# Moving two feed-forward products ahead of the output product, with features and tokens taken in another order

## The chip, the cores and the metric

The kernel runs on one core of one Trainium2 chip. Its time is the device time of one execution in microseconds (us); a kernel's time is the median of its runs. The engines have short names here: PE (TensorE) multiplies matrices, and PEld is its loading of stationary operands; DVE (VectorE) and ACT (ScalarE) do elementwise work; POOL (GpSimd) does a little elementwise work and issues the DMAs that add to what is there; SP (SyncE) issues plain DMAs.

## What is computed

One sequence of 512 tokens with 1024 features passes through four layers. Each is a mixer (RWKV-7, windowed attention, a gated spatial unit, gated linear attention, in this order) and a feed-forward network (FFN), each behind a norm and added to the stream h; a last norm ends the program.

```
for i in range(4):
    h = h + mixer[i](rmsnorm(h, norm_mix[i]))
    h = h + swiglu(rmsnorm(h, norm_ffn[i]), ffn_w_in[i], ffn_w_out[i])
return rmsnorm(h, norm_final)

swiglu(x, w_in, w_out):  gate, up = split(x @ w_in);  (silu(gate) * up) @ w_out
```

The hidden width of the FFN is 2816. All data are float32.

## The kernel before

**Precision.** A float32 operand is split into a high part (an ACT cast, tile `whi` for weights) and a remainder (a DVE subtraction, tile `wlo`), and each product is three matmuls in a faster format: high by high, high by remainder, remainder by high (`mm3`, line 540). Weights arrive in raw tiles `wraw` (eight buffers), and there are three buffers each for `whi` and `wlo`.

**Where results lie.** h lies by token, four blocks of 128 tokens by 1024 features. A product's result lies in PSUM, which has eight banks of 128 x 512.

**The FFN.** The hidden width is cut into six blocks, four of 512 and two of 384 (`WIDTHS`, line 28), and blocks are taken in pairs (`PARTS`, line 27). For each pair, `ffn` (line 705) computes two hidden blocks (`hidden`, line 803) and then the output product that takes this pair's hidden values into h (`out_fast`, line 727). Both use `seven` (line 740), a scheme that computes a 2 x 2 block product with seven products instead of eight, out of sums of quarters of the operands. In the order in which they are written they are m1, m2, m5, m6, m3, m7, m4. Each has four token-and-feature subtiles, that is 24 matmuls in a block with four row tiles; the output product of the 384 pair has three row tiles and 18. The sums of weight quarters are made by the DMA that loads: POOL issues a DMA that adds onto a raw tile. m5, m6 and m4 use one raw pair that is added to three times in turn; m3 and m7 use another that is added to once, between them, after m3's high part and remainder are made. m1's accumulator, two banks, stays in use until m4 is done. The quarter sums of the input are made by DVE in `combine`.

**After an output.** When the last output product of an FFN, or a mixer's output projection (`out_proj`, line 851), has finished two token blocks of one half of the features, `finish` (line 583) sums squares on ACT, transposes the blocks on PE and scales them into the next stage's operand. In an FFN, features 0 to 511 of tokens 256 to 511 are finished last, by m4. A mixer's projections (`gemm`, line 546, and `gemm_tok`, line 559) sum over eight feature tiles of 128 in order from 0 to 7; `gemm_tok` takes its weights two row tiles at a time, and for each pair goes over the four token blocks. `rstd` (line 669) turns the sums of squares into the factor of the norm, with twelve small DVE operations on a 128 x 4 tile; `store` (line 1599) does this once at the end, scales eight tiles and issues eight stores from SP.

**What sets the order.** All calls are first recorded (`Program.record`), and then `Program.run` (line 287) lays them out. Going forward in time by its own prices (`price`, line 262), it gives each engine the earliest recorded instruction that can start within 60 ns of the earliest start; a tile's buffer is given only if work recorded earlier keeps enough. Order of recording is thus priority. Each engine's queue is then fixed, and runs in that order. Where PE would stand idle, `keep_warm` (line 391) puts in products of the identity, called fillers here; they are recorded at line 453 and write a bank that nobody reads. Line 233 is the line of every other instruction.

Of the kernel before, what the change touches and what calls it, by code (L numbers as in the profile page):

```python
# [25 lines left out]
SLOTS = 48  # L26
PARTS = ((0, 1), (2, 3), (4, 5))
WIDTHS = (512, 512, 512, 512, 384, 384)
# [408 lines left out]
class K:  # L437
# [3 lines left out]
    def __init__(self, prog, d, es):  # L441
# [15 lines left out]
        self.hp = self.pool("hp", 4, side="right")  # L457
        self.kind = "plain"

    def pool(self, name, bufs, es=None, **kw):  # L460
# [85 lines left out]
    def gemm(self, w, x, evac, ncol=P):  # L546


        nk = len(x)
        ps = self.bank()  # L550
        for k0 in range(0, nk, 8):
            n = min(8, nk - k0)
            hi, lo = self.weights(w[:, k0 * ncol:(k0 + n) * ncol], n, ncol)
            for k in range(n):
                xh, xl = x[k0 + k]
                self.mm3(ps[:ncol], hi[:, k, :], lo[:, k, :], xh, xl, k0 + k == 0, k0 + k == nk - 1)
        evac(ps)

    def gemm_tok(self, w, c0, x, evac):

        ps = [self.bank() for _ in range(NB)]
        v = w.rearrange("(k p) n -> p k n", p=P)
        nk = len(x)
        for k0 in range(0, nk, 2):
            hi, lo = self.weights(v[:, k0:k0 + 2, c0:c0 + S], 2, S)
            for b in range(NB):
                t = slice(b * P, (b + 1) * P)
                for k in range(2):
                    xh, xl = x[k0 + k]
                    self.mm3(ps[b], xh[:, t], xl[:, t], hi[:, k, :], lo[:, k, :], k0 + k == 0, k0 + k == nk - 1)  # L570
        for b in range(NB):
            evac(b, ps[b])
# [95 lines left out]

    def rstd(self, spread=True, acc=None):

        nc = self.nc
        ms = self.sm.tile([P, NB], F32, name="ms")
        if acc is None:
            ss = self.ss.rearrange("p (b n) -> p b n", b=NB)
            nc.vector.tensor_add(ms, ss[:, :, 0], ss[:, :, 1])
        else:
            ps = self.bank()
# [3 lines left out]
        nc.vector.tensor_scalar(ms, ms, 1.0 / D, EPS, op0=ALU.mult, op1=ALU.add)  # L681
        col = self.sm.tile([P, NB], F32, name="rcol")
        self.rsqrt(col, ms)
        if not spread:
            return col, None
        ps = self.bank()
        for b in range(NB):
            nc.tensor.transpose(ps[:, b * P:(b + 1) * P], col[:, b:b + 1].to_broadcast([P, P]), self.ident)
        bc = self.slot()
        nc.vector.tensor_copy(bc, ps)  # L690
        return col, bc

    def operand(self):
        return self.nf if self.nf else self.nx

# [9 lines left out]
    def ffn(self, i, g_next):  # L705


        nc, d = self.nc, self.d
        col, _ = self.rstd(spread=False)
        neg = self.sm.tile([P, NB], F32, name="ncol")  # L710
        nc.vector.tensor_scalar(neg, col, -1.0, None, op0=ALU.mult)
        x = self.operand()
        self.begin(g_next)
        for n, part in enumerate(PARTS):
            gs = {}
            for kh, j in enumerate(part):
                W = WIDTHS[j]
                w = d['ffn_w_a'][i, j] if j < 4 else d['ffn_w_b'][i, j - 4]
                self.hidden(w, W, x, col, neg, gs, kh)
            w = d['ffn_o_a'][i, n] if n < 2 else d['ffn_o_b'][i]  # L720
            self.out_fast(w, W // P, lambda key: self.left_of(gs, key), n == len(PARTS) - 1)

# [80 lines left out]
    def hidden(self, w, W, x, col, neg, gs, kh):  # L803


        nc = self.nc
        got, gate = {}, {}
# [20 lines left out]
        for name, ps in self.seven(w, W, lambda key: x[key]):  # L828
# [20 lines left out]
        give(got['m7'], 1)  # L849
# [749 lines left out]
    def store(self):  # L1599

        nc = self.nc
        col, _ = self.rstd(spread=False)
        for b in range(NB):
            for nh in range(2):
                c = slice(nh * S, nh * S + S)
                o = self.slot()
                if nh:
                    nc.scalar.activation(o, self.h[b][:, c], AF.Identity, scale=col[:, b:b + 1])
                else:
                    nc.vector.tensor_scalar(o, self.h[b][:, c], col[:, b:b + 1], None, op0=ALU.mult)  # L1610
                nc.sync.dma_start(self.d['out'][b * P:(b + 1) * P, c], o)

# [30 lines left out]
def arrays(inputs):  # L1643
# [28 lines left out]
    part = lambda w, p: quarters(w, (starts[p[0]], starts[p[1]]), (0, S), S)  # L1672
    a['ffn_o_a'] = np.stack([np.stack([part(w, p) for p in PARTS[:2]]) for w in w_out])
    a['ffn_o_b'] = np.stack([part(w, PARTS[2]) for w in w_out])
    rkv = a.pop('rw_w_rkv')[0]
# [74 lines left out]
```

## Time and profile before

| | |
|---|---|
| runs: median (range) | 2699.64 us (2697.85 to 2700.97, three runs) |
| the profiled execution | 2696.06 us, span 2694.4 us |
| PE busy | 2577.9 us, fillers included |
| DVE, ACT, POOL busy | 1825.4, 1380.2, 465.8 us |
| mean granted clock of TensorE | 0.99 |
| read from memory | 359.51 MB, 134 GB/s over the span |

The FFNs lie at about 560 to 890, 1095 to 1400, 1740 to 2060 and 2330 to 2680 us. A row of operations by time has start, duration, engine, line, operation, result and operands, and in brackets the idle time before it and what ended that. A row of a window has its bounds, its length, and then for each engine asked for its busy time and number of instructions, then the granted clock, the share of the DMA engines' time and GB/s. A filler leaves two records. Matmuls are pipelined: one starts about 0.23 us (512 columns) after the one before, and its record lasts 0.39 us.

### The profile page before, as it was taken

The numbers are of one execution on the slowest core, as the hardware profiler recorded it, in microseconds if no ns is written. First come the engines' busy times: TensorE is split into PE (matmuls) and PEld (weight loads), VectorE is DVE, ScalarE is ACT, GpSimd is POOL, SyncE is SP. The second block draws the span as 40 slices with busy tenths as digits, with TensorE's granted clock in tenths as the row PEclk, the third lists the DMA queues.
The fourth block names the chain that finished last, engine by engine and source line by source line (L and its number), as shares of the span: only waits on it lengthen the run. The fifth ranks groups of instructions, "written<-read, shape, count | busy, mean of one in ns | idle before, by whom it ended". The sixth has DMA issues, their size and how long they took to land. (4 is left out here: it accounts for less than half of the span.)

```text
span 2694.4 us, 35601 instructions
## 1 busy us (share of the span) xinstructions
PE 2577.9 (96%) x13324; PEld 2118.2 (79%) x13324; DVE 1825.4 (68%) x2804; ACT 1380.2 (51%) x2304; POOL 465.8 (17%) x492
## 2 busy tenths in 40 slices
PE   8999799999999999999999999999999999999997
PEld 7677678878779766788797888878788777877896
DVE  8687786577577875675768465567677635567767
ACT  4545443365555555565555232555556633555654
POOL 1022343311112243111122000011112000011121
PEclk9999999999999999999999999999999999999999
DMA  3210001268888532588896222388888221398885
GB/s 129 75 57 14 4 9 51 97 157 197 210 188 195 133 96 69 132 200 211 189 214 173 103 91 89 94 196 198 201 184 191 102 86 55 105 222 204 196 197 124
DMA packets 127149, 366.29 MB, mean 136 GB/s; under 512 B 13424, under 2 KB 20976, under 8 KB 126976
## 3 DMA queue, kind: packets, MB, share of 16 engines
q0 software_dynamic: 41472, 138.43, 28.8%
q1 hardware_dynamic: 85504, 225.59, 24.6%
q8 instruction: 105, 1.72, 0.3%
q14 instruction: 68, 0.56, 0.1%
HBM read 359.51 MB, written 2.10 MB: 134 GB/s over the span
## 5 line engine op out<-in xcount | busy, mean ns | idle before, releaser
L233 PE MATMUL ps<-whi,slot 128*128 128x512 f32 (+1 forms) x5072 | 1556.2, 384 | 28.7 <-ACT whi L233 20.5
L233 PEld LDWEIGHTS ps<-whi,slot 128*128 128x128 f32 x5072 | 944.7, 189 | 196.1 <-ACT whi L233 28.4
L233 DVE TENSOR_TENSOR wlo<-wraw,whi 128x1024 fp32r<-128x1024 f32 (+2 forms) x628 | 727.1, 1161 | 548.3 <-ACT whi L233 544.4
L233 ACT CAST whi<-wraw 128x1024 fp32r<-128x1024 f32 (+2 forms) x632 | 626.9, 993 | 741.6 <-PE ps L233 543.3
L233 PE MATMUL ps<-wlo,slot 128*128 128x512 f32 (+1 forms) x2536 | 975.9, 385 | 17.0 <-DVE wlo L233 16.5
L233 PEld LDWEIGHTS ps<-wlo,slot 128*128 128x128 f32 x2536 | 478.6, 189 | 108.6 <-DVE wlo L233 30.2
L233 POOL DMA_DIRECT2D wraw<-ffn_w_a x128 | 109.2, 860 | 1097.7 <-DMA wraw<-ffn_w_a 579.4
L233 PE MATMUL ps<-slot,whi 128*128 128x512 f32 (+2 forms) x864 | 274.6, 396 | 2.0 <-ACT slot L233 1.9
L233 DVE TENSOR_TENSOR slot<-slot 128x512 fp32r<-128x512 f32 (+5 forms) x369 | 234.4, 662 | 26.8 <-ACT slot L233 24.8
L233 PEld LDWEIGHTS ps<-slot,whi 128*128 128x128 f32 (+2 forms) x864 | 157.0, 185 | 47.6 <-issue 6.2
L233 PE MATMUL ps<-slot,wlo 128*128 128x512 f32 (+2 forms) x432 | 169.7, 393 | 0.0
L233 ACT CAST slot<-slot 128x512 fp32r<-128x512 f32 (+1 forms) x240 | 136.9, 603 | 60.4 <-DVE slot L233 52.0
L233 ACT COPY left<-ps 128x512 f32<-128x512 f32 (+1 forms) x196 | 108.4, 554 | 69.2 <-PE ps L233 68.9
L233 DVE TENSOR_TENSOR h<-h,ps 128x512 f32<-128x512 f32 x168 | 112.5, 683 | 21.2 <-PE ps L233 20.3
L453 PE MATMUL ps<-ident 128*128 128x128 f32 x670 | 103.5, 295 | 1.7 <-POOL ident L233 1.4
L233 POOL DMA_DIRECT2D wraw<-ffn_o_a x64 | 54.5, 851 | 282.5 <-DVE wlo L233 191.2
L233 ACT COPY slot<-ps 128x512 f32<-128x512 f32 (+2 forms) x137 | 71.0, 565 | 60.2 <-PE ps L233 59.9
L453 PEld LDWEIGHTS ps<-ident 128*128 128x128 f32 x670 | 93.9, 203 | 9.2 <-POOL ident L233 1.4
L233 PEld LDWEIGHTS ps<-slot,wlo 128*128 128x128 f32 (+2 forms) x432 | 79.7, 184 | 20.7 <-issue 2.5
L233 POOL DMA_DIRECT2D wraw<-ffn_w_b x64 | 54.9, 860 | 215.6 <-DVE wlo L233 140.7
L233 DVE TENSOR_TENSOR slot<-ps,slot 128x128 fp32r<-128x128 f32 (+2 forms) x95 | 35.5, 415 | 62.9 <-PE ps L233 46.0
L233 DVE SCALAR_TENSOR_TENSOR left<-left,ncol 128x512 f32<-128x512 f32 (+1 forms) x96 | 65.8, 702 | 10.3 <-ACT left L233 10.2
(258 smaller groups left out, 2497.6 us busy)
## 6 DMA issues: line engine op xcount, KB each, us to landing
wraw<-ffn_w_a SPq DMA_DIRECT2D x128, 512.0 KB, 4.7
wraw<-ffn_w_a POOLq DMA_DIRECT2D x128, 512.0 KB, 5.7
wraw<-ffn_o_a SPq DMA_DIRECT2D x64, 512.0 KB, 5.3
wraw<-ffn_o_a POOLq DMA_DIRECT2D x64, 512.0 KB, 5.6
wraw<-ffn_w_b SPq DMA_DIRECT2D x64, 384.0 KB, 3.8
wraw<-ffn_w_b POOLq DMA_DIRECT2D x64, 384.0 KB, 6.0
wraw<-ffn_o_b SPq DMA_DIRECT2D x16, 512.0 KB, 5.5
wraw<-ffn_o_b POOLq DMA_DIRECT2D x16, 512.0 KB, 5.9
```

The source lines that it names most:

```text
L233: op = self.add(eng.name, lambda: getattr(eng.target, what)(*map(real, args), **{k: real(a) for k, a in kw.items()}), *self.price(eng.name ...
L453: self.nc.tensor.target.matmul(self.ps.tile_pool.tile([P, S], F32, name="ps")[:, :P], self.ident.real(), self.ident.real(), start=True, st ...
```

## The change

All parts concern order; no operation on large tiles is added or removed. Outside TensorE's fillers the only new instructions are a second copy of the last norm's small operations.

- The pair of 384-wide blocks becomes the first pair of each FFN (`PARTS`); the weight arrays are laid out to match.
- `hidden` becomes a generator that yields after each of its seven products. `ffn` runs a pair's two blocks to the end, then the first two products (m1, m2) of the next pair's first block, and only then the output product; the other five follow it.
- `gemm` and `gemm_tok` take the feature tiles 4 to 7 first and 0 to 3 last, if their operand is the one made by the stage before (`order`).
- In the last column half of a mixer's `out_proj`, with at least four row tiles, the last two weight pairs are taken together: token block 0 through all four row tiles, then block 1, and so on. The last projection of the RWKV mixer has two row tiles and keeps its order.
- `rstd` is cut in two, and `store` makes the norm's factor, scales and stores for tokens 0 to 255 and then for tokens 256 to 511.

```
-PARTS = ((0, 1), (2, 3), (4, 5))
+PARTS = ((4, 5), (0, 1), (2, 3))
...
+    def order(self, x):
+        n = len(x)
+        return [(k + n // 2) % n for k in range(n)] if x is self.nx or x is self.op else list(range(n))
...
     def gemm_tok(...):
+        ks = self.order(x)
+        runs = [ks[i:i + 2] for i in range(0, len(ks), 2)]
+        if late:
+            runs = [[r] for r in runs[:-2]] + [runs[-2:]]
+        else:
+            runs = [[r] for r in runs]
+        for run in runs:
+            parts = [(r, self.weights(v[:, r[0]:r[0] + 2, c0:c0 + S], 2, S)) for r in run]
             for b in range(NB):
                 t = slice(b * P, (b + 1) * P)
+                for r, (hi, lo) in parts:
+                    for j, k in enumerate(r):
+                        xh, xl = x[k]
+                        self.mm3(ps[b], xh[:, t], xl[:, t], hi[:, j, :], lo[:, j, :], k == ks[0], k == ks[-1])
...
     def ffn(self, i, g_next):
+        for m, (n, kh, gs, steps) in enumerate(blocks):
+            for _ in steps:
+                pass
+            if kh:
+                if m + 1 < len(blocks):
+                    for _ in range(2):
+                        next(blocks[m + 1][3])
+                w = d['ffn_o_a'][i, n - 1] if n else d['ffn_o_b'][i]
+                self.out_fast(w, WIDTHS[PARTS[n][0]] // P, lambda key: self.left_of(gs, key), n == len(PARTS) - 1)
...
     def out_proj(self, w, x, last=True):
-            self.gemm_tok(w, nh * S, x, ev)
+            self.gemm_tok(w, nh * S, x, ev, last and nh == 1 and len(x) >= 4)
...
     def store(self):
-        col, _ = self.rstd(spread=False)
-        for b in range(NB):
+        for half in range(2):
+            col = self.rcol(half * 2, half * 2 + 2)
+            for j in range(2):
+                b = half * 2 + j
```

More of the change, by code (lines that the diff above doesn't have):

```diff
@@ L713, in ffn @@
         self.begin(g_next)
+        blocks = []
         for n, part in enumerate(PARTS):
@@ L1601, in store @@
         nc = self.nc
-        col, _ = self.rstd(spread=False)
-        for b in range(NB):
[L1604 to L1611, printed above, removed]
+        for half in range(2):
+            col = self.rcol(half * 2, half * 2 + 2)
+            for j in range(2):
+                b = half * 2 + j
+                for nh in range(2):
+                    c = slice(nh * S, nh * S + S)
+                    o = self.slot()
+                    if nh:
+                        nc.scalar.activation(o, self.h[b][:, c], AF.Identity, scale=col[:, j:j + 1])
+                    else:
+                        nc.vector.tensor_scalar(o, self.h[b][:, c], col[:, j:j + 1], None, op0=ALU.mult)
+                    nc.sync.dma_start(self.d['out'][b * P:(b + 1) * P, c], o)
 def consts():
```

59 lines of the change are left out of this document (28 added, 31 removed).

## The prediction

> **What bounds the kernel now.** I read the page first, then busy time by stage, then TensorE's (PE's) timeline around each stretch in which it waits, then the vector engine's (DVE's) timeline there.
>
> ```profile
> PE 2577.9 (96%) x13324; PEld 2118.2 (79%) x13324; DVE 1825.4 (68%) x2804; ACT 1380.2 (51%) x2304; POOL 465.8 (17%) x492
> ...
> L453 PE MATMUL ps<-ident 128*128 128x128 f32 x670 | 103.5, 295 | 1.7 <-POOL ident L233 1.4
> ...
> 540.00:885.00 345.00, 335.77 (x1634) 286.20 (x1633) 243.98 (x318) 202.14 (x298) 56.52 (x67) 0.99 0.81 191
> 885.00:1075.00 190.00, 178.18 (x845) 126.57 (x844) 133.63 (x255) 106.31 (x294) 67.41 (x57) 0.99 0.33 91
> 1075.00:1395.00 320.00, 310.66 (x1473) 261.10 (x1472) 215.24 (x269) 179.38 (x250) 50.42 (x60) 0.99 0.79 188
> 2330.00:2681.00 351.00, 339.75 (x1640) 288.19 (x1639) 255.04 (x332) 204.44 (x298) 59.76 (x70) 1.00 0.78 180
> ```
>
> PE bounds every stage; nothing else is near its span. But the first row flatters it: the L453 row is filler, products of the identity that line 453 puts into planned waits (670 records, two per filler, so 335). What can be won is idle time plus filler. The change does the same real matmuls with the same operands, so only those stretches can move. Before 540 us (the RWKV mixer) both kernels have the same PE order. After it, four kinds of stretch carry the prediction.
>
> **Output products waiting for summed weights.** Part boundary of the first FFN (start, duration, engine, operation, idle before and what ended it):
>
> ```profile
> 672.88 0.39 PE L233 MATMUL ps<-whi,slot 128*128 128x512 f32 x1
> ...
> 673.10 1.05 PE L453 MATMUL ps<-ident 128*128 128x128 f32 x8
> ...
> 673.61 1.04 ACT L233 CAST whi<-wraw 128x1024 fp32r<-128x1024 f32 x1 [1.45 <-DMA wraw<-ffn_o_a]
> ...
> 674.71 0.73 PE L233 MATMUL ps<-whi,slot 128*128 128x512 f32 x2 [0.55 <-ACT whi L233]
> ...
> 678.50 0.39 PE L233 MATMUL ps<-whi,slot 128*128 128x512 f32 x1
> ...
> 680.03 0.73 PE L233 MATMUL ps<-whi,slot 128*128 128x512 f32 x2 [0.47 <-ACT whi L233]
> ...
> L233 POOL DMA_DIRECT2D wraw<-ffn_o_a x64 | 54.5, 851 | 282.5 <-DVE wlo L233 191.2
> ...
> wraw<-ffn_o_a POOLq DMA_DIRECT2D x64, 512.0 KB, 5.6
> ```
>
> PE waits from 673.27 to 674.71 and from 678.89 to 680.03, 2.6 us, and between each cast and its remainder (wlo) another 0.9 and 0.5: 4.0 us. The cause is the accumulating DMA that makes the weights of product m7 out of those of m3. Six such boundaries (the windows 672 to 683, 796 to 808, 1210 to 1221, 1334 to 1345, 1854 to 1865, 1980 to 1991) have in all 67.00 - 57.16 = 9.8 us idle and 19.5 of filler, which overlaps the product before each burst; at 4.0 each they are 24. The two of the last FFN cost far less:
>
> ```profile
> sum 67.00, PE 57.16; mean PE 9.53
> ...
> sum 67.00, PE 19.52; mean PE 3.25
> ...
> 2430.00:2460.00 30.00, 28.97 (x127) 1.00 0.80 163
> 2550.00:2580.00 30.00, 29.41 (x133) 1.00 0.81 168
> ...
> 2430.00:2460.00 30.00, 0.38 (x2) 1.00 0.80 163
> 2550.00:2580.00 30.00, 1.21 (x8) 1.00 0.81 168
> ```
>
> That is 1.0 idle and 0.4 filler, 0.6 and 1.2: about 1.0 us each once overlap is taken off, for the same work.
>
> *After.* Two products of the next block (48 matmuls) stand ahead of each output product, so output weights load and are summed that much earlier. In the changed order the second boundary of FFNs 0 to 2 has the matmul order that the last FFN has now (four matmuls of m3 slipped behind the first two of m6): I take 1.0 us, saving 3.0 x 3 = 9. The first boundary now belongs to the narrow pair, whose output product has 18 matmuls. From one m3 remainder to the m7 cast is 1.2 (wlo) + 0.85 (POOL issue) + 5.6 + 1.05 = 8.7 us; m6 and m3 cover 36 x 0.227 = 8.2 there and 48 x 0.227 = 10.9 in a wide one. I take 2.0, saving 2.0 x 3 = 6. Together -15, between 0 (the wait moves with the product) and -20 (all near zero). The Trainium skill ("DMA: Bandwidth & Descriptors", Anatomy of one DMA) fits a DMA issued from GpSimd as 2.0 us plus bytes over 436 GB/s, 3.2 us for 512 KB. The row has 5.6, and the row decides; by the fit the narrow boundary would save 3.0 as well and the sum below be 3 us lower.
>
> **Mixer starts.** Windows 885 to 925, 1395 to 1450, 2040 to 2110, all PE work, then filler alone; below them, the granted clock (third number from the end) after three stalls:
>
> ```profile
> sum 165.00, PE 156.95; mean PE 52.32
> ...
> sum 165.00, PE 13.20; mean PE 4.40
> ...
> 568.30:571.70 3.40, 3.37 (x8) 2.71 (x9) 3.40 (x6) 0.00 (x0) 0.00 (x0) 0.50 0.43 154
> ...
> 896.00:899.30 3.30, 3.30 (x15) 3.00 (x14) 3.30 (x7) 0.65 (x2) 1.29 (x2) 0.50 0.57 112
> 1753.00:1756.40 3.40, 2.57 (x11) 2.12 (x12) 3.40 (x7) 0.22 (x1) 0.00 (x0) 1.00 0.40 131
> ```
>
> 8.1 idle + 13.2 filler, about 18 us without overlap. PE waits there for features 0 to 3 of tokens 256 to 511, which the FFN's last product m4 finishes. Taken last, they leave 12 of the 24 matmuls of a projection (2.7 us) as cover, more with the next projection's first half. The changed order has 15 fillers at these places where this one has 40; in proportion 18 becomes 7: -11, between 0 and -15.
>
> **FFN starts.** The second FFN's:
>
> ```profile
> 1104.19 2.84 PE L453 MATMUL ps<-ident 128*128 128x128 f32 x24
> 1109.62 0.50 PE L233 MATMUL ps<-wlo,slot 128*128 128x512 f32 x1 [2.59 <-DVE wlo L233]
> ...
> 1098.26 3.83 DVE L233 TENSOR_TENSOR slot<-slot 128x512 f32<-128x512 f32 x6
> ...
> 1108.35 1.22 DVE L233 TENSOR_TENSOR wlo<-wraw,whi 128x1024 fp32r<-128x1024 f32 x1
> ...
> 2443.21 0.62 PE L233 MATMUL ps<-whi,slot 128*128 128x512 f32 x2
> ...
> 2443.89 0.62 PE L233 MATMUL ps<-whi,slot 128*128 128x512 f32 x2
> ...
> 851.18 0.51 PE L233 MATMUL ps<-whi,slot 128*128 128x384 f32 x2
> ...
> 851.70 0.51 PE L233 MATMUL ps<-whi,slot 128*128 128x384 f32 x2
> ```
>
> DVE works 10 us without a break on sums of input quarters, and only then on the remainder that m2 needs; PE stands 5.3 us, some 25 over the four FFNs. Both DVE order and stall remain after the change, but the block in front is narrow: three matmuls take 0.52 us instead of 0.68, so the 26 to 36 of m1 and m2 ahead of the stall cover 1.4 to 1.9 less. Against that, splitting the last four weight rows by token block completes the first two token blocks 12 matmuls (2.7 us) earlier in three of the four mixers, and DVE's sums can begin sooner. I take +1.0 each, +4, between -2 and +11 (1.9 each and a half-clock window of 1.7 at two).
>
> **The narrow pair right after the start.** It has three quarters of the matmul time to hide the same quarter sums. The changed order has 9, 7, 5 and 0 fillers inside it; at this boundary 14 fillers went with 4.0 us, 0.29 each: +6. The narrow pair at the end of an FFN has waits without filler that go:
>
> ```profile
> 829.75 0.83 ACT L233 CAST whi<-wraw 128x768 fp32r<-128x768 f32 x1 [2.01 <-DMA wraw<-ffn_w_b]
> ```
>
> This one holds PE some 1.9 us in the first FFN; I take 1 us in each of three: +3 in all, between 0 and +10.
>
> **Last FFN and tail.** Its boundaries get worse (fillers 1 to 8 and 4 to 5 in the order): +2 and +1. The final output product is wide now; the end costs 36.00 - 31.05 = 5.0 idle plus 3.1 filler, and I take 5 afterwards: -3. Sum 0, between -4 and +6.
>
> ```profile
> 2645.00:2681.00 36.00, 31.05 (x144) 1.00 0.41 70
> ...
> 2645.00:2681.00 36.00, 3.10 (x22) 1.00 0.41 70
> ...
> 2685.84 0.16 DVE L233 SCALAR_TENSOR_TENSOR rcol<-rs_t,rcol 128x4 f32<-128x4 f32 x1
> 2686.04 2.56 ACT L233 ACTIVATE slot<-h,rcol 128x512 f32<-128x512 f32 x4 [3.01 <-DVE rcol L233]
> ...
> 2686.55 4.48 SPq L233 DMA_DIRECT2D out<-slot  x8
> ```
>
> Eight stores take SP 4.48 us after the norm; with the first half's four issued during m4, 2.2 go, at least the 1.3 of two of the four scalings: -2. The second copy of the norm's twelve small DVE operations (about 0.2 us each) stands in the order behind the last remainders but one, beside PE work; without that cover it would cost 2.4.
>
> **Moved instructions elsewhere.** Loads of the next block's m1 and m2 go ahead of the output weights on SP; eight raw buffers allow it because the earlier block frees four by then. On POOL the sums keep their order. The next block's accumulators hold two of eight PSUM banks through the output product, which itself needs six.
>
> **Sum.** -15 - 11 + 4 + 3 + 0 - 2 = -21. A second estimate: 38 fillers fewer in the order at 0.29 us is -11, with the tail -13. The planner lays its order out for a 512 KB transfer of 1.1 + 1.5 + 1.5 = 4.1 us (lines 362 to 364), the row has 5.6, so stretches without a planned filler will also wait; I take the middle, -17. Against the profiled execution (2696.06 us, span 2694.4) that is 2679. That execution was 3.6 us quicker than the median of the runs, 2699.64, so for the median I say 2683. About 0.2% (5.4 us) is what a measurement can tell from no change.
>
> **Rivals.** *The narrow block in front costs more than all gains* (slower). For: DVE's chain is 11 us long and only half of it shows now; a shorter block exposes more. Per FFN: 2.5 for 48 matmuls at 0.053 less, 1.7 for a half-clock window, 5 of DVE's backlog, 9; times 4 is 36 against gains of 28: 2708. It decides from 7 us per FFN on. Against: DVE is at 71% in the FFNs and catches up. Chance 0.15.
>
> *The boundary wait re-forms* (no change). If m7's wait follows the product wherever it stands, because m7 comes directly after m3 and the chain of 8.7 us is untouched, the 15 go and with the same discount 2697 remains. For: the chain's length; against: the last FFN's 1.0 us. Chance 0.11.
>
> *The clock drops more often* (smaller gain). The rows above show the granted clock at 0.50 for 3.4 us after stalls at 568 and 896; such windows cost 1.7 us each. With fewer fillers and longer starts, four more make 2690. Against: the stall at 1748 is as long and left the clock at 1.00. Chance 0.06. The Trainium skill ("TensorE: Matmul & The Clock Gate", What's actually happening) says that a free-running window of about 3.4 us without enough activity halves the clock; the trace agrees in length and rate, and the phase of the window is left to luck.
>
> **Chances.** 0.68 for the forecast, whose own range is 2674 to 2692. Faster 0.74 (forecast and clock), same 0.11, slower 0.15. The range 2671 to 2698 leaves out the slower case and a little below.
>
> **What would show it.** Right: FFN boundaries of FFNs 0 to 2 with one or two short waits in place of four; 896's stall gone; four stores at the end. Wrong: FFN starts over 8 us, waits with DVE as releaser through the narrow pair, or m7 still waiting for ffn_o weights.

## The result, and the profile after

The changed kernel took 2721.3 us (median; 2718.91 to 2730.99), the kernel before 2700.3 beside it (2697.85 to 2701.08): a ratio of 1.0086, with a 95% interval from 1.0060 to 1.0113. It is slower by 0.9%, where the prediction had 0.6% faster. The profiled execution took 2723.45 us with a span of 2721.7, 27.3 more than that of before.

From the page of the changed kernel (busy time; the filler's group; median landing of the adding DMAs):

```profile
PE 2583.0 (95%) x13248; PEld 2118.6 (78%) x13248; DVE 1823.9 (67%) x2816; ACT 1379.0 (51%) x2304; POOL 462.1 (17%) x492
...
L453 PE MATMUL ps<-ident 128*128 128x128 f32 x594 | 95.8, 303 | 1.7 <-POOL ident L233 1.4
...
wraw<-ffn_o_a POOLq DMA_DIRECT2D x64, 512.0 KB, 6.5
...
wraw<-ffn_o_b POOLq DMA_DIRECT2D x16, 512.0 KB, 7.6
```

There are 38 fillers fewer, as the order said, but PE is idle for longer, and the adding DMAs of the output product land 0.9 and 1.7 us later than the 5.6 and 5.9 of before. The stretches of the prediction, in the changed kernel: the three mixer starts (windows of the same lengths as before, all PE work and then filler alone), and then the four FFN starts (the first 12 us behind each norm):

```profile
sum 165.00, PE 157.62; mean PE 52.54
...
sum 165.00, PE 5.00; mean PE 1.67
...
sum 48.00, PE 33.49; mean PE 8.37
...
sum 48.00, PE 17.58; mean PE 4.39
```

The same 12 us in the kernel before:

```profile
sum 48.00, PE 36.45; mean PE 9.11
...
sum 48.00, PE 15.12; mean PE 3.78
```

At the mixer starts 8.2 us of filler went and idle time hardly changed. The FFN starts have 3.0 us more idle and 2.5 more filler. Behind them, the four first boundaries, where the narrow pair's output product lies (windows with PE busy and clock, then their sums, then the sum of the filler):

```profile
655.00:666.00 11.00, 6.54 (x27) 0.91 1.01 217
1195.00:1206.00 11.00, 6.73 (x28) 0.88 0.99 217
1846.00:1857.00 11.00, 5.99 (x24) 0.76 1.01 217
2445.00:2458.00 13.00, 8.26 (x37) 0.87 0.95 195
sum 46.00, PE 27.52; mean PE 6.88
...
sum 46.00, PE 5.54; mean PE 1.39
```

46.00 - 27.52 = 18.5 us idle, the clock below 1.00 in each, and the DMA engines busy throughout (a share of 0.95 to 1.01). One of them from close by, by timeline: POOL's queue, then the ACT cast, then PE, then the clock in the 3.4 us after the stall (a window with all engines; the third number from its end is the granted clock):

```profile
648.84 0.86 POOL L233 DMA_DIRECT2D wraw<-ffn_w_a  x1 [9.32 <-DVE wlo L233]
650.08 0.84 POOL L233 DMA_DIRECT2D wraw<-ffn_w_a  x1 [0.39 <-DVE slot L233]
653.53 0.86 POOL L233 DMA_DIRECT2D wraw<-ffn_o_b  x1 [2.60 <-DVE wlo L233]
...
662.86 1.04 ACT L233 CAST whi<-wraw 128x1024 fp32r<-128x1024 f32 x1 [4.43 <-DMA wraw<-ffn_o_b]
...
663.95 1.22 PE L233 MATMUL ps<-whi,slot 128*128 128x512 f32 x2 [4.22 <-ACT whi L233]
...
664.00:667.40 3.40, 3.40 (x8) 2.72 (x9) 3.40 (x6) 0.00 (x0) 1.26 (x2) 0.50 0.60 106
```

The two DMAs from `ffn_w_a` are the next block's sums for m5, recorded after the whole output product; the planner puts them on POOL's queue between the output's sums for m5 and those for m6. The output's own sum is issued at 653.53, and the ACT cast that reads it starts 9.3 us later. PE waits 4.22 us at the first matmul of m6, without a filler inside, and runs at half clock afterwards.

To set kernels side by side I use one measure, the gap time: from the end of a real matmul to the start of the next, fillers counted as idle, gaps over 0.15 us only. It is given by place in the four FFNs together, counted from the norm's first operation: the start (to 12 us), the first pair (12 to 80), its output and boundary (80 to 150), the second pair and boundary (150 to 275), and the rest. The last column is the time for which the trace's clock records show half clock after 540 us, the tail left out; a microsecond of it costs up to half a microsecond (8 matmuls stand in the window above, at 0.50, and 16 in the 3.4 us behind it, at 1.00).

| | start | first pair | first boundary | second | rest | FFNs | whole program | half clock |
|---|---|---|---|---|---|---|---|---|
| before | 25.2 | 4.7 | 14.2 | 17.0 | 26.4 | 87.5 | 173.8 | 13.7 |
| changed | 30.8 | 12.9 | 28.0 | 16.4 | 16.5 | 104.5 | 190.8 | 37.5 |

So 17.0 us of the 27.3 is gap time. Another 3.7 lie ahead of anything that was changed: the first FFN's norm starts at 560.0 us instead of 556.3, behind a stretch of 13.65 us at half clock at 244 us that this execution has and that of before has not. The 6.6 left fit the 23.8 us more at half clock behind 540 us. The column "rest" holds the end of each FFN and the start of the next mixer: of its -9.9, 5.4 are the mixer starts (17.6 to 12.2), and 4.5 the end of the FFNs, where the narrow pair had its stalls. More came at the front.

### The profile page after: what moved, and what is told of

Same layout as the page of the kernel before. It is cut to its first block, busy times and chain, and to the rows that moved or that the text cites. A ratio compares the mean times of both kernels' runs of the same rounds, so it can differ in the third digit from the quotient of the medians.

```text
span 2721.7 us, 35438 instructions
## 1 busy us (share of the span) xinstructions
PE 2583.0 (95%) x13248; PEld 2118.6 (78%) x13248; DVE 1823.9 (67%) x2816; ACT 1379.0 (51%) x2304; POOL 462.1 (17%) x492
## 3 DMA queue, kind: packets, MB, share of 16 engines
q0 software_dynamic: 41472, 138.43, 28.4%
## 4 chain that ended last, share of the span: by engine, by line
PE 43%; DMA 6%; issue 5%; DVE 5%; ACT 2%; POOL 1%; ACTq 0%; POOLq 0%; DVEq 0%
PE ps L233 43%; DMA wraw<-ffn_w_a 2%; DMA wraw<-ffn_o_a 2%; DVE slot L233 2%; DVE wlo L233 1%; ACT whi L233 1%; POOL wraw L233 1%; DMA wraw<-ffn_w_b 1%; DMA wraw<-ffn_o_b 1%; ACT slot L233 1%; DVE left L233 0%; DVE mx L233 0%; PE ps L453 0%; DVE h L233 0%; ACT left L233 0%
## 5 line engine op out<-in xcount | busy, mean ns | idle before, releaser
L233 DVE TENSOR_TENSOR slot<-slot 128x512 fp32r<-128x512 f32 (+6 forms) x369 | 235.0, 663 | 31.9 <-ACT slot L233 28.5
L233 ACT CAST slot<-slot 128x512 fp32r<-128x512 f32 (+1 forms) x240 | 137.6, 603 | 53.5 <-DVE slot L233 44.2
L453 PE MATMUL ps<-ident 128*128 128x128 f32 x594 | 95.8, 303 | 1.7 <-POOL ident L233 1.4
L233 PEld LDWEIGHTS ps<-slot,wlo 128*128 128x128 f32 (+2 forms) x432 | 79.6, 184 | 20.5 <-issue 2.5
L453 PEld LDWEIGHTS ps<-ident 128*128 128x128 f32 x594 | 86.0, 210 | 7.4 <-POOL ident L233 1.4
```

The lines of the kernel that those rows point to most:

```text
L233: op = self.add(eng.name, lambda: getattr(eng.target, what)(*map(real, args), **{k: real(a) for k, a in kw.items()}), *self.price(eng.name ...
L453: self.nc.tensor.target.matmul(self.ps.tile_pool.tile([P, S], F32, name="ps")[:, :P], self.ident.real(), self.ident.real(), start=True, st ...
```

## The experiments

Each batch ran beside the kernel before on one chip; ratios are to that kernel, with their 95% intervals. Its median was 2705.64 us in the first batch (a wide spread, 2693.80 to 2715.64), which had the first three kernels told here and the changed kernel with POOL in recorded order, so times expected there in us are best read as ratios.

**One part at a time.** First each part of the change left out, or done alone. Without the products ahead (changed kernel):

```diff
-                if m + 1 < len(blocks):
-                    for _ in range(2):
-                        next(blocks[m + 1][3])
```

> The changed kernel, but each output product comes straight after its own pair of blocks again; the narrow pair stays first, and the other parts stay. Queue theory (the next block's first weight sums stand on POOL between the first and second sums of the output product, and with their loads delay these by some 4 us at each of eight boundaries, after which the clock halves): the single 4 us stalls vanish, the boundaries cost what they cost before, and the time falls by 10 to 18 us to 2703 to 2711. Narrow-block theory (the pair put first exposes DVE's backlog and costs the time): the time stays at 2715 or more.

With the narrow pair last again (changed kernel):

```diff
-PARTS = ((4, 5), (0, 1), (2, 3))
+PARTS = ((0, 1), (2, 3), (4, 5))
```

> The changed kernel with the narrow pair last again; the two products ahead and the other parts stay. Queue theory: the stalls of 4 us at the eight boundaries stay, FFN starts return to 5.3 us and the narrow pair's stalls go, so 2705 to 2715. Narrow-block theory: below before, 2680 to 2695.

The kernel before with only the products ahead, then with only the narrow pair in front, then with only features, tokens and norm halves:

```diff
 # only the products ahead
+                if m + 1 < len(blocks):
+                    for _ in range(2):
+                        next(blocks[m + 1][3])
 # only the narrow pair in front
-PARTS = ((0, 1), (2, 3), (4, 5))
+PARTS = ((4, 5), (0, 1), (2, 3))
 # only features, tokens, halves
+        return [(k + n // 2) % n for k in range(n)] if x is self.nx or x is self.op else list(range(n))
...
+            self.gemm_tok(w, nh * S, x, ev, last and nh == 1 and len(x) >= 4)
...
+        for half in range(2):
```

> The kernel before with one part of the change alone: the next block's first two products ahead of each output product. Queue theory: slower than before by 6 to 16 us, 2706 to 2716, with stalls of about 4 us ended by DMA wraw<-ffn_o_a. Narrow-block theory and the prediction's own steps: faster, 2685 to 2692.

> The kernel before with only the narrow pair put in front in each FFN. No product is moved ahead, features and tokens are in the old order, the norm is in one piece. Theory that the narrow block costs by itself (three matmuls in 0.52 us cover 0.16 less of the same sums than three in 0.68, at FFN starts that were 5.6 us longer in all, and in the pair behind): 1.003 to 1.006, with FFN starts of 7 us and more and waits on DVE behind them. Theory that it costs only together with the products moved ahead, because the narrow block's output product is the shortest (six wide weights in place of eight) and its sums are caught by the next block's loads: 0.999 to 1.002, with the boundaries behind the narrow pair no longer than the 8 us of before.

> The kernel before with only the two smaller parts of the change: late features and late tokens taken last, and the last norm in halves. No product is moved ahead and the narrow pair stays last. The mixer starts were 17.6 us in the kernel before and 12.2 in the changed one, and the tail's stores start earlier. Theory that the two other parts make the whole loss and that these two help: 0.997 to 0.999, faster by 3 to 8 us. Theory that any re-ordering of the program by a planner with a wrong price loses: 1.000 to 1.004.

| | median, us | ratio | interval |
|---|---|---|---|
| changed, without the products ahead | 2715.90 | 1.0039 | 1.0018 to 1.0060 |
| changed, narrow pair last | 2706.26 | 1.0005 | 0.9988 to 1.0022 |
| before + products ahead | 2710.68 | 1.0023 | 1.0002 to 1.0045 |
| before + narrow pair in front | 2720.73 | 1.0052 | 1.0030 to 1.0073 |
| before + features, tokens, halves | 2703.64 | 0.9991 | 0.9974 to 1.0008 |

Two parts lose: the narrow pair in front most, the products ahead as well (its interval just clears 1). Features, tokens and halves are not told from zero. The three parts alone add up to 0.66%, most of the 0.86%. As ratios, the theories of the first three kernels were half right: without the products ahead the time is at the upper end of the queue theory's range (1.001 to 1.004), the products ahead alone at the lower end of it (1.002 to 1.006), and the narrow pair last falls between the two theories (1.002 to 1.005, and 0.993 to 0.998). The narrow pair alone was expected at 1.003 to 1.006 by the theory that it costs by itself, and it does. In the kernel before a wide pair stands first; its four windows of 98 us, from 12 us behind each norm, have 392.00 - 386.51 = 5.5 us idle (PE, then filler):

```profile
sum 392.00, PE 386.51; mean PE 96.63
...
sum 392.00, PE 0.38; mean PE 0.10
```

With only the narrow pair moved there (the same windows; then the first FFN: an ACT cast that waits for a sum, PE's wait for the copy that stands behind this cast on ACT, a later wait of PE, and PE at the pair's output product):

```profile
sum 392.00, PE 367.86; mean PE 91.97
...
sum 392.00, PE 17.75; mean PE 4.44
...
592.68 0.83 ACT L233 CAST whi<-wraw 128x768 fp32r<-128x768 f32 x1 [4.87 <-DMA wraw<-ffn_w_b]
...
593.94 0.44 PE L233 MATMUL ps<-whi,slot 128*128 128x384 f32 x1 [2.84 <-ACT left L233]
...
610.33 0.41 PE L233 MATMUL ps<-ident,left 128*128 128x128 f32 x2 [0.85 <-DVE left L233]
...
651.25 1.22 PE L233 MATMUL ps<-whi,slot 128*128 128x512 f32 x2 [2.65 <-ACT whi L233]
```

24.1 us idle, and 17.4 more filler. The narrow pair is shorter, so the windows take in its output product too. In the first 68 us of each, the pair itself, 12.4 us are idle (5.0 in before); the rest lies at that output product, whose first m6 matmul waits 2.0 to 3.3 us in each FFN for a sum of `ffn_o_b`, with none of the next block's sums in front. In the pair, ACT waits 4.87 us for a summed weight tile. The page of the kernel before has what a narrow block must hide (median landing):

```profile
wraw<-ffn_w_a POOLq DMA_DIRECT2D x128, 512.0 KB, 5.7
...
wraw<-ffn_w_b POOLq DMA_DIRECT2D x64, 384.0 KB, 6.0
```

A sum of 384 KB lands no sooner than one of 512 KB (6.0 against 5.8 with the pair in front, too), while three matmuls take 0.52 us instead of 0.68: a quarter of the cover goes, none of the wait. How much of the 12.4 us this makes is not shown; some of the waits are DVE's.

**The place of all sums on POOL's queue.** The theory after the first look at the trace: the next block's sums between the output's make the stall, and POOL in recorded order cures it.

```diff
+        sums = [op for op in ops if op.eng == "POOL" and op.lat == 2000.0][::-1]
...
+                    if e == "POOL" and op.lat == 2000.0 and op is not sums[-1]:
+                        continue
```

> The changed kernel with one rule added to the planner: POOL's adding DMAs go in the order in which they were recorded, so the next block's sums stand behind all sums of the output product. Queue theory in its narrow form (place on POOL's queue): the 4 us stalls go and the time falls to 2695 to 2708. If the loads of the next block, which still run on the DMA engines beside the sums, are what makes the sums land late: stalls stay near 4 us, 2713 or more. Narrow-block theory: unchanged, 2717 or more.

It took 2733.02 us, 1.0095 (1.0064 to 1.0126). The stall behind the narrow pair did shrink (gap time from 80 to 110 us: 23.6 to 11.5), but waits came up elsewhere, and the FFNs had 107.6 us of gap time in place of 104.5. In this form the theory fell. The same edit on the kernel before, and on the kernel before with features, tokens and halves:

> The kernel before with one change in the planner: POOL takes its adding DMAs in the order in which they are recorded, so that the sums for m7 stand before those for m4. In the kernel before each boundary of the first three FFNs has 4.0 us of short waits at m7, where m7's sums stand on POOL behind m4's (order b, b, b, b, c, c), and the last FFN, with b, b, c, b, b, c, has 1.0. Theory that this place on the queue makes those waits: each of the six boundaries falls by 2 to 3 us and the ratio is 0.994 to 0.998. Theory that a forced order only moves the waits, as it did in the changed kernel (1.0095 there): 0.999 to 1.004.

> The kernel before with late features and late tokens taken last, the last norm in halves, and POOL's adding DMAs in the order in which they are recorded. Nothing is moved ahead and the narrow pair stays last. Theory that the two helping parts and the order of the sums add up: 0.993 to 0.997, the version that beats both kernels. Theory that the forced order only moves waits: 0.998 to 1.003.

They came to 1.0018 (0.9992 to 1.0043) and 0.9987 (0.9964 to 1.0010). Recorded order is no better than the planner's. The place of m7's sums behind m4's, which one theory blames for the 4.0 us waits of before, costs nothing that these runs could tell.

**The planner's price.** In the changed kernel the adding DMAs move 138.43 MB in 28.4% of 16 engines' span, 179 GB/s (28.8% and 178 in the kernel before); the planner has 360.

```diff
-                dma = max(dma, s + 1100.0) + max(450.0, op.columns / 360.0)
+                dma = max(dma, s + 1100.0) + max(450.0, op.columns / (178.0 if e == "POOL" else 360.0))
```

> The changed kernel, with one number of the planner's pricing changed: an adding DMA on POOL's queue is priced at 178 bytes per ns (138.43 MB in 28.8% of the span of the engines, from the table of queues of the changed kernel) in place of 360; SP's loads stay at 360. The planner then puts out-product matmuls later or fillers before them, where it took a sum for landed that was not. Theory that the change loses by stalls which the planner does not see, because its price for adding DMAs is too low: the idle time between TensorE's matmuls without fillers falls, the half-clock windows behind the boundaries go, and the ratio is 1.000 to 1.005. Theory that the bytes themselves are late at the boundaries, whatever order is written: the stalls stay, only filled, 1.004 to 1.008. Theory that the narrow block in front costs by DVE's chain at the FFN starts: 1.007 to 1.010, unchanged.

1.0095 (1.0076 to 1.0114). That is in the range of the third theory, but not for its reason: the waits in the narrow pair went (first pair 1.2 us of gap time), and the first boundary grew from 28.0 to 44.2. The first two theories fall. POOL's queue shows what happened: at the first boundary of three FFNs four of the next block's sums now stand between the output's, where the changed kernel has two. The planner does count each transfer behind the one issued before it (`dma` in the line above). What it doesn't weigh, when it hands POOL the next sum, is which of two is waited for sooner: it takes the one that can start first. A more honest price doesn't mend that.

**The clock.** Fourteen more fillers ahead of the first m6 matmul at the eight boundaries (the marks are set where `out_fast` and `hidden` are recorded), and the changed kernel again:

```diff
+            if op.mark and self.warm[0].slots["ps"].free:
+                for _ in range(14):
+                    self.warm[1]()
```

> The changed kernel with fourteen identity products (fillers) more right before the first m6 matmul of each output product but the last of an FFN, eight places, where TensorE stood 2.6 to 6.0 us without a filler in the changed kernel. Nothing else is moved. Theory that the throttle takes part of the loss (a stall without fillers is followed by 3.41 us at half clock): the half-clock windows right behind these eight places go, the stalls themselves stay as long as they are, and the ratio to the kernel before falls from 1.0086 to 1.004 to 1.006, 5 to 10 us. Theory that only the length of the stalls counts, and that the half-clock windows are where they would be anyway: 1.0075 to 1.010, since a filler that is not done when the sum lands costs up to 0.3 us at each place.

> The changed kernel once more, unaltered, on the same chip as the three beside it, and with more rounds than the four runs it had. Every theory expects 1.006 to 1.010. Its ratio less that of the kernel with fillers at the boundaries (1.0044) is what those fillers are worth: the clock theory expects 0.002 to 0.005; a ratio here of 1.005 or less would say that the first four runs were high and the fillers are worth nothing. The half-clock window of 13.65 us at 244 us, in a part where the order is that of the kernel before, does not come again if it was chance.

1.0044 (1.0026 to 1.0062) with them, 1.0076 (1.0047 to 1.0105) without; span and mean granted clock of the two profiled executions:

```profile
core 0: 2716.3 us, clock 0.989
...
core 0: 2734.9 us, clock 0.978
```

Time at half clock after 540 us is 20.5 us with the fillers, 68.3 in this execution without and 37.5 in the first one, with the same order. Gap time is no smaller (193.9 against 191.9 and 190.8). Over all runs the median granted clock is 0.988 in the nine with the fillers, and 0.980 and 0.984 in the seven and four without (0.987 in the kernel before). The fillers cut the half clock, then; the intervals overlap, so that they are worth about 0.3% is likely but not shown. The half-clock window at 244 us came back here, as 17.07 us, in a part where nothing was changed; other kernels have it or not, and its cause stays open.

**The next block's sums taken away.** The same PE order but for one filler, without the 16 adding DMAs that stand between the output's sums; in those blocks m5, m6 and m4 read a quarter without the other added. And the same 16 left out of the kernel before, as a control:

```diff
-        add(b, 0)
+        if not self.ahead:
+            add(b, 0)
```

> The changed kernel without the first adding DMAs (the sums for m5) of the two FFN blocks per FFN whose first two products go ahead: 16 adding DMAs of 512 KB fewer in all, eight pairs, each of which stands on POOL's queue between the output product's two sums. Left out of the computation: in those blocks m5, m6 and m4 read quarter 2 without quarter 0 added, so the hidden values are others. TensorE's order is the changed kernel's but for one filler. Theory that this pair of sums makes the stall at the output's first m6 matmul (by its place on the queue and by the bandwidth it takes): the output's second sums are issued 2 to 4 us earlier and land in 5 to 7 us in place of 7.5 to 10, idle time at the first boundary falls from 23.6 us over four FFNs to 8 to 14, at the second from 15.3 to 8 to 12, and the ratio comes to 1.000 to 1.004. Theory that the chain from m5's split over the second sum to m6 is too long by itself once nothing wide stands between (the narrow pair's output has three units in place of four): first boundaries stay above 17 us, the ratio 1.005 to 1.009.

> The kernel before without the same 16 adding DMAs (the sums for m5 in the second and third block pair of each FFN, first half). Left out of the computation: there m5, m6 and m4 read quarter 2 without quarter 0 added. It is the control for the changed kernel without them, which went from 1.0076 to 0.9977 on one chip. Theory that the 16 sums cost only where they stand between the output's sums: here, where they stand behind them, their absence is worth little, 0.998 to 1.001. Theory that 16 adding DMAs fewer are worth 20 us wherever they stand: 0.990 to 0.994.

The changed kernel without them: 0.9977 (0.9957 to 0.9996), beside 1.0076 on the same chip. The kernel before without them: 1.0004 (0.9986 to 1.0022). So the 16 sums cost nothing that shows where they stand in before, and 1.0% where they stand in the changed kernel, a little more than either theory had. The first boundaries without them (windows at the same places, PE, then filler), and the landing of the output's sums in 25 us around the first of them:

```profile
sum 46.00, PE 41.08; mean PE 10.27
...
sum 46.00, PE 5.43; mean PE 1.36
...
wraw<-ffn_o_b POOLq DMA_DIRECT2D x3, 512.0 KB, 5.6
```

18.5 us idle have become 4.9, and the sums land in 5.6 where the changed kernel has 7.7 in such a window.

**Their place alone.** Nothing left out; those eight pairs are held behind the output's sums for m6 and m7, and nothing else is tied:

```diff
+                    if op.hold and not op.hold.done:
+                        continue
...
+            self.ahead = m > 0 and kh == 0
+            self.held = self.sums[-3] if self.ahead else None
...
+                if self.ahead and q == 0:
+                    o.hold = self.held
```

> The changed kernel with one thing different: the first adding DMAs (the sums for m5) of a block whose m1 and m2 went ahead may be put on POOL's queue only after the output product's sums for m6 and m7. Nothing is left out; TensorE's order is the same but for one filler, and all other sums keep their places; what moves is eight pairs of adding DMAs, three to five places back on one queue. Theory that the place of these sums makes the loss: idle time at the first boundaries falls from 23.6 to 8 to 13 us as without the sums (8.5 there), fewer half-clock windows follow, the ratio comes to 0.998 to 1.002. Theory that it is the bytes: the stalls only move to m7 and to the next block's m5, as with all sums forced into order, the ratio stays at 1.005 to 1.009.

0.9997 (0.9977 to 1.0016), against 1.0076 and 1.0086 unheld in other batches: the place is worth 0.8%. In the first FFN POOL's queue is now as follows (line 234 here is line 233 above), and PE waits 1.18 us where it waited 4.22; the last two rows are a second wait, told below:

```profile
647.69 0.86 POOL L234 DMA_DIRECT2D wraw<-ffn_o_b  x1 [14.29 <-DVE wlo L234]
...
658.64 2.08 POOL L234 DMA_DIRECT2D wraw<-ffn_w_a  x2
...
655.06 0.73 PE L234 MATMUL ps<-whi,slot 128*128 128x512 f32 x2 [1.18 <-ACT whi L234]
...
660.56 1.03 POOL L234 DMA_DIRECT2D wraw<-ffn_o_b  x1
...
674.95 0.51 PE L234 MATMUL ps<-whi,slot 128*128 128x512 f32 x1 [2.97 <-ACT whi L234]
```

The output's m6 sum is issued no earlier. It follows the norm's first operation by 647.69 - 553.6 = 94.1 us here and by 653.53 - 560.0 = 93.5 in the changed kernel. It lands sooner (6.2 us after its issue instead of 9.2), because the next block's two sums are not under way ahead of it. What was wrong was not POOL's waiting but the transfers in front. PE's waits did not all go. The pair now stands ahead of the output's last sum, one of m4's, issued at 660.56: it lands 13.6 us later, behind the two, and PE waits for it (3.0 us here and 4.7 in the third FFN). So gap time fell by 6.4 us only (190.8 to 184.4). The clock can make up the rest: what it takes away (one less the mean granted clock, times the span, averaged over the runs) is 34.8 us with the sums held, and 44.9 and 53.4 in the two sets of runs without.

**Both remedies.** The narrow pair last, and the sums held:

> The changed kernel with the narrow pair last again, as in the kernel before, and with the sums of the block ahead held back behind the output's sums for m6 and m7. Nothing is left out. With the narrow pair last but without holding it was 1.0005. Theory that the narrow pair in front and the place of these sums are the two causes of the loss and that the rest of the change helps: 0.994 to 0.998, faster than both kernels. Theory that products ahead cost for another reason (they take from the next block the work that its own sums were hidden by, idle time 11.6 us late in the blocks in place of 2.4): 0.999 to 1.002.

> The version with the narrow pair last and the sums of the block ahead held back, once more and unaltered, because its 0.9917 stood on six runs and its profiled execution (span 2691.2) was only 3 us under the one of the kernel before. If it is a gain: 0.990 to 0.996. If those six runs were low by chance: 0.996 to 1.000.

0.9917 (0.9892 to 0.9943), and once more 0.9928 (0.9903 to 0.9954): this version beats both kernels, and the first time by more than either theory had. With the narrow pair last no output sum is left behind the held pair, so that part of what this gains over 0.9997 may be the place of m4's sum again. The gain over before is not the clock (medians 0.9865 and 0.987 over its two sets of runs, 0.986 and 0.987 over those of before beside them), and gap time has fallen by 10.0 of some 19 us; the rest is open. How much of it are the products ahead? The kernel before with them alone and their sums held:

> The kernel before with only the two products ahead of each output product, and with the sums of the block ahead held back behind the output's sums for m6 and m7; narrow pair last, features and tokens in the old order, the norm in one piece. Without holding, the two products ahead alone were 1.0023. Theory that the place of the sums is all that was wrong with them: 0.993 to 0.998, most of the gain of the version with both remedies. Theory that the gain comes from features, tokens and norm (0.9991 by themselves) and holding only takes a loss away: 0.998 to 1.001.

0.9942 (0.9922 to 0.9963), where without holding it was 1.0023: the greater part, if not all (0.9928 in the same batch). Last, the version with both remedies, held behind the output's last recorded sum, one of m4's, in place of m7's:

```diff
-            self.held = self.sums[-3] if self.ahead else None
+            self.held = self.sums[-1] if self.ahead else None
```

> As the version with the narrow pair last and the sums held back, but held until the output's last sums, those for m4, too. Theory that each sum of the next block costs only while an output sum is still to be issued: 0.990 to 0.996, the same or 2 us better. Theory that holding them so long makes the next block's own m5 wait (DMAs in a burst, 8 to 10 us each): 0.996 to 1.000.

It was 1.0127 (1.0101 to 1.0152), and neither theory saw why. The planner issues m4's sums ahead of m7's last one, so this edit doesn't hold the pair longer but lets it in front of that last sum. POOL and ACT at the first boundary, with both remedies:

```profile
686.15 0.86 POOL L234 DMA_DIRECT2D wraw<-ffn_o_a  x1 [2.08 <-DVE wlo L234]
686.69 2.11 POOL L234 DMA_DIRECT2D wraw<-ffn_w_a  x2
...
692.87 2.00 ACT L234 CAST whi<-wraw 128x1024 fp32r<-128x1024 f32 x2 [4.19 <-DMA wraw<-ffn_o_a]
```

And with the pair one place further ahead, with PE and the clock behind it:

```profile
683.52 2.11 POOL L234 DMA_DIRECT2D wraw<-ffn_w_a  x2
685.92 0.86 POOL L234 DMA_DIRECT2D wraw<-ffn_o_a  x1 [0.29 <-DVE wlo L234]
...
700.13 1.04 ACT L234 CAST whi<-wraw 128x1024 fp32r<-128x1024 f32 x1 [8.95 <-DMA wraw<-ffn_o_a]
...
701.22 1.22 PE L234 MATMUL ps<-whi,slot 128*128 128x512 f32 x2 [8.20 <-ACT whi L234]
...
696.70:707.00 10.30, 5.78 (x16) 4.72 (x17) 1.91 (x2) 1.04 (x1) 0.00 (x0) 0.50 0.46 163
```

The same sum, one of m7's, issued within 0.3 us of the same time, is ready 700.13 - 685.92 = 14.2 us later instead of 6.7. The transfers of this queue land one behind the other: the pair at 692.36 and 696.17, then the sum at 700.03. PE stands 8.20 us, and 10.2 us at half clock begin within this stall. PE's order around m4 and m7 shifts with it, so that not all of the 2% is this one swap, but its stall is there at each first boundary (first boundaries 33.3 us of gap time in place of 9.2).

All in the measure from above:

| | start | first pair | first boundary | second | rest | FFNs | whole program | half clock |
|---|---|---|---|---|---|---|---|---|
| before + narrow pair in front | 31.0 | 17.2 | 20.7 | 14.4 | 14.3 | 97.6 | 186.4 | 30.7 |
| changed, narrow pair last | 24.9 | 4.1 | 15.9 | 14.4 | 32.9 | 92.1 | 178.1 | 34.1 |
| changed, 16 sums left out | 30.8 | 16.2 | 13.3 | 9.6 | 14.8 | 84.7 | 171.4 | 30.7 |
| before, 16 sums left out | 25.3 | 2.8 | 15.5 | 17.2 | 26.9 | 87.6 | 173.3 | 13.7 |
| changed, sums held | 30.9 | 19.4 | 23.2 | 8.8 | 14.9 | 97.2 | 184.4 | 23.9 |
| both remedies | 24.9 | 4.8 | 9.2 | 12.6 | 26.9 | 78.3 | 163.8 | 23.9 |
| before + products ahead, sums held | 25.0 | 6.5 | 8.3 | 10.2 | 31.6 | 81.5 | 165.9 | 23.9 |
| the pair one place ahead | 24.9 | 4.4 | 33.3 | 22.3 | 26.9 | 111.8 | 196.9 | 85.3 |

## Why the prediction was wrong

- **The step that failed: the boundaries, and in them the sentence "On POOL the sums keep their order".** They do not. At eight places the next block's sums for m5 go between the output's sums, since with m1 and m2 ahead their raw tiles are loaded and read early enough. The -15 (-12 with the last FFN's +3) became about +13 (28.0 + 16.4 of gap time at the first two boundaries in place of 14.2 + 17.0), and each first stall lies open, with half clock behind it. That is some 25 of the 36 us between the forecast without its tail (-19) and the 17.0 of gap time. Some 4 of the 13 come with the narrow pair alone (20.7 + 14.4). With the sums held, the products ahead alone took 12.7 us off these boundaries (8.3 + 10.2) and gave 0.9942; -15 would be 0.9944. The mechanism, output weights summed earlier behind two products, was right, then, and holds only where nothing else is sent to the same queue in front.
- **The narrow pair right after the start, +3, and the FFN starts, +4.** The starts cost 5.6. The pair behind has 8.2 more gap time in the changed kernel (forecast +6) and 12.5 when it is moved alone; the end of the FFNs gives back 4.5 (forecast 3). In gap time these terms were near, then. What the forecast had wrong is the pair's own output product: it took 2.0 us off this boundary in three FFNs, and even with the pair moved alone PE waits there at m6 (20.7 us in place of 14.2). The rival "the narrow block in front costs more than all gains" had the direction, with 36 us as its price. Alone the pair costs 0.5%, 14 us, and with the sums held at most 0.8%, 22 us (0.9997 against 0.9917 in one batch). It named the right engine of PE's waits only at the starts; behind them it is mostly the weights' sums, whose 6.0 us stood on the page, while the +6 was counted from planned fillers. The Trainium skill ("DMA: Bandwidth & Descriptors", Anatomy of one DMA) has a fixed part of 2.0 us plus bytes over 436 GB/s; an estimate by that is 3.2 us for 512 KB and 2.9 for 384. The rows agree that a smaller sum is hardly quicker, and not with the level: 5.7 and 6.0 here, up to 14.2 behind two others.
- **"The clock drops more often", 0.06.** It came together with the stalls instead of in place of the forecast: 37.5 and 68.3 us at half clock after 540 us against 13.7. The execution of before was a lucky one there; over whole sets of runs the clock takes 44.9 and 53.4 us from the changed kernel and 34 to 36 from the kernel before. Fewer fillers were counted as a gain; part of them had stood in stalls that are still there, and a stall without them can cost the clock as well.
- **Mixer starts, -11: -5.4** (gap time 17.6 to 12.2). The filler went, 8.2 us of it, as the order said; the idle time beside it stayed, 8.1 to 7.4. Nor is it mainly the order of the features: by the same measure features, tokens and halves alone leave 16.6, and the narrow pair in front alone, which ends each FFN with a wide output product, leaves 13.2. The step "Taken last, they leave 12 of the 24 matmuls of a projection" has little to show for itself.
- **Last FFN and tail, -2 by the halves.** From PE's last matmul to the end it is 10.0 us instead of 12.8 (11.4 with only features, tokens and halves). Right, and too small to be told in the runs.
- **"The boundary wait re-forms".** That is nearest to what happened, but at m6 rather than m7, and longer than it was.
- **The second estimate, fillers counted in the planned order,** gave -13 with the tail. 261 fillers stand in the version at 1.0005 and also, with the pairs moved a few places on POOL, in the one at 0.992. The count does not see a late transfer.

## What to carry to other kernels

When work is moved ahead, follow also what it sets free to be issued early: list each DMA queue's order after the change, and look for transfers that slip in front of one that is waited for sooner. A transfer that is not urgent cost nothing that shows behind the urgent one and several microseconds in front of it, so order the queue by who waits first, and hold back only the offenders; forcing the whole queue into one order cost as much as it gave. And put small blocks where their transfers have cover, as a block with a quarter less work didn't have a quarter less transfer time.

## What was not expected of the hardware

- An adding DMA of 384 KB lands in 6.0 us (median of 64), one of 512 KB in 5.7 (of 128), in the same execution of the kernel before; by plain DMAs from SP they are 3.8 and 4.7.
- Two adding DMAs of 512 KB issued 2 us earlier make the next one on that queue ready in 14.2 us instead of 6.7.
- The same instruction order had 37.5 us at half clock after 540 us in one execution and 68.3 in another, with spans 13 us apart; a gain of 0.2% can't be read from one profile of this kernel.
- Up to the first FFN's norm PE's order is the same in all kernels, and their profiled executions reach it at 551.4 to 562.5 us. The seven that reach it at 559.2 or later are those with 13.65 or 17.07 us at half clock from about 244 us on.
